# Attention in a hybrid decoder: another order of scores and turns, rotary angles on GpSimd, and x tiles between the first weights

## The chip, the cores and the metric

The kernel runs on one core of a Trainium2 chip. The metric is the device time of one execution in microseconds; the median of the runs is compared. A core has TensorE (PE in the profile), VectorE (DVE), ScalarE (ACT), GpSimd (POOL) and SyncE (SP). Each runs its own program in order, and semaphores make one wait for another. DMA transfers are issued from an engine's queue.

## The reference

Two layers over 512 positions of width 1024, all in float32. Layer 0 mixes by sliding-window attention, layer 1 by a gated delta rule; each is followed by a gated feed-forward part. The change lies in layer 0 alone:

```python
def swa_sink_attention(u, w_in, q_gain, k_gain, sinks, w_out, cos, sin):
    qkv = u @ w_in                                    # 16 query, 4 key, 4 value heads of 64
    q = partial_rope(rms_norm(q, q_gain), cos, sin)   # rotary on the first 16 of 64 dims
    k = partial_rope(rms_norm(k, k_gain), cos, sin)
    # blocks of 128 queries against their own and the previous block of keys, window 128
    scores = einsum("bnqhgd,bnkhd->bnhgqk", qb, kb) * (hd ** -0.5)
    probs = softmax(concatenate([masked scores, sink]))[..., :-1]
    return einsum("bnhgqk,bnkhd->bnqhgd", probs, vb) @ w_out
```

The angles of the rotary part are position times frequency, reduced to one period before the sine.

## The kernel before

**Matmuls.** A dense product in float32 is made of three matmuls (`mm3`, L148 to L150), with weights and activations each split in a rounded part and its remainder. `weight` loads a weight tile on SP's queue (L136), rounds it on ScalarE (L137, `whi`) and takes the remainder on VectorE (L138, `wlo`); there are three buffers of each. [...]

**Start.** `run` loads h in eight tiles of 128x512, h0 and h1 from ScalarE's queue and the others from SP's (L1131), and the first weight group W0 as four halves of 128x512, also from SP's. `norm_split` scales each tile by the gain on ScalarE (L192) and takes the remainder on VectorE (L193); squares for the normalisation follow on ScalarE (L180, L183). Some warm-up matmuls (L1128) stand ahead on TensorE.

**Attention.** `attn` runs six dense groups c = 0 to 5 over the weights win: c = 0 makes the keys, c = 3 the values, the others the queries of a key head each. Every group needs its own `weight` tiles. After the group its `post` normalises it and applies the rotary factors cc and sn (`qk_norm`), and turns it on TensorE (L427). The factors come from `attn_setup` and `rope`, called behind the dense loop of c = 0: 43 small instructions of 128x32 on VectorE between the cast of the positions and the sine, then three sine instructions on ScalarE (L332, L333) with a table load ahead.

**Lanes.** Two lanes, one behind the other, take two key heads each. For a block n of 128 queries and a key head, `attn_scores` makes the scores S of its four query heads on TensorE (L515), masks and maximises them on VectorE (L518), takes exponentials on ScalarE (L524), and scales them by the reciprocal sum, two heads on VectorE and two on GpSimd (L528). `attn_turn` turns these on TensorE (T, L537) and copies them to SBUF on ScalarE (L539). `attn_values` multiplies both heads' results with the values (V, L546). Block 0 has 128 keys, the others have 256. Lane 0 interleaves with the dense groups c = 2 to 5 and lane 1 with the output products of lane 0 (128x512).

**What sets the order.** The lanes are generators that the dense loops call by `pump`. A scheduler of the framework then gives each engine its final order by its own estimates, so that the program's order is not quite that of the code. DMAs from SP and ScalarE use eight semaphores in turn; the ninth waits until the first has landed.

Of the kernel before, what the change touches and what calls it, by code (L numbers as in the profile page):

```python
# [10 lines left out]
F32 = mybir.dt.float32  # L11
# [3 lines left out]
ALU = mybir.AluOpType  # L15
# [4 lines left out]
NB = 4  # L20
# [50 lines left out]
class Builder:  # L71
# [56 lines left out]
    def weight(self, src, cols=1024, parts=1):  # L128
# [134 lines left out]
    def rope(self):  # L263
        nc = self.nc
        n = NB * 8
        V = nc.vector
        new = lambda: self.ax.tile([P, n], F32, tag="ra", name="ra", bufs=10)
        pos = self.ax.tile([P, NB], I32, name="pos", bufs=1)
        nc.sync.dma_start(pos, self.ins["pos"])
        fr = self.ax.tile([P, 8], F32, name="fr", bufs=1)  # L270
        nc.sync.dma_start(fr, self.ins["freq"].partition_broadcast(P))
# [17 lines left out]
        def wrap(r, k):  # L289
            for cc in (c1, c2, c3):  # L290
                V.scalar_tensor_tensor(r, k, -cc, r, op0=ALU.mult, op1=ALU.add)

        def times(a, power):
            c = float(np.remainder(2.0 ** power, tp))
            if power == 22:
                c = 2.0 ** 22 - tp * np.floor(2.0 ** 22 / tp)
            hi = np.floor(c * 512) / 512
            mid = np.floor((c - hi) * 2 ** 21) / 2 ** 21
            k = nearest(a, c / tp)
            r = new()  # L300
            V.tensor_scalar(r, a, float(hi), None, op0=ALU.mult)
            V.scalar_tensor_tensor(r, k, -c1, r, op0=ALU.mult, op1=ALU.add)
            V.scalar_tensor_tensor(r, k, -c2, r, op0=ALU.mult, op1=ALU.add)
            V.scalar_tensor_tensor(r, a, float(mid), r, op0=ALU.mult, op1=ALU.add)
            V.scalar_tensor_tensor(r, k, -c3, r, op0=ALU.mult, op1=ALU.add)
            V.scalar_tensor_tensor(r, a, float(c - hi - mid), r, op0=ALU.mult, op1=ALU.add)
            return r
# [3 lines left out]
        V.scalar_tensor_tensor(B, A, -4096.0, ang, op0=ALU.mult, op1=ALU.add)  # L311
        a1 = nearest(A, 1.0 / 1024)
        a0 = new()
        V.scalar_tensor_tensor(a0, a1, -1024.0, A, op0=ALU.mult, op1=ALU.add)
# [81 lines left out]
    def attn(self, h, after):  # L396
# [38 lines left out]
        def lane(i):  # L435


            sc, pT = {}, {}
            for x in range(NB + 2):
                if x >= 2:  # L440
                    while "v" not in ready:
                        yield 0.5
                    n = x - 2
                    if n == 0:
                        ao[i] = [(self.a2(), self.a2()) for _ in range(4)]
                    po = self.psum()
                    both = [pT.pop((n, j)) for j in range(2)]
                    for b in range(len(both[0])):
                        for j in range(2):
                            self.attn_values(n, 2 * i + j, both[j], v, po, b)  # L450
                    for g in range(4):
                        s = slice(n * P, (n + 1) * P)
                        hi, lo = ao[i][g]
                        self.split(po[:, g * P:(g + 1) * P], hi[:, s], lo[:, s])
                    if n == NB - 1:
                        ready.add(("o", i))
                        return
                    yield 1
                for j in range(2):
                    kv = 2 * i + j  # L460
                    if x < NB:
                        while kv not in ready:
                            yield 0.5
                        sc[x, j] = self.attn_scores(x, kv, qT[kv], kT[kv])
                        yield 0.5
                    if 1 <= x < NB + 1:
                        pT[x - 1, j] = self.attn_turn(x - 1, sc.pop((x - 1, j)))
                        yield 0.5
# [4 lines left out]

        for c in range(6):
# [12 lines left out]
            if c == 0:  # L487
                self.attn_setup()
# [628 lines left out]
    def run(self, stages):  # L1117
# [12 lines left out]
        for m in range(KT):  # L1130
            (nc.scalar if self.first and m < 2 else nc.sync).dma_start(h[m], self.ins["xT"][m])  # L1131
            if self.first and m in (0, 1):
                self.W0 = (self.W0 if m else []) + [self.weight(self.ins["win"][0, m], 1024, 2)]
            if self.first:
                self.norm_split(h[m], m, gains[stages[0]])
            else:
                self.norm_tile(h[m], m, gains[stages[0]])
        nc.sync.dma_start(self.ident, self.ins["ident"])
# [39 lines left out]
```

## Time and profile before

| | us |
|---|---|
| median of three runs | 1492.2 (1490.68 to 1493.09) |
| profiled execution | 1490.9 |
| its span | 1489.0 |
| TensorE busy | 1468.6 |
| VectorE busy | 915.1 |
| ScalarE busy | 635.9 |
| GpSimd busy | 72.1 |

The span is the time from the first to the last record of the profile. TensorE is busy 99% of it, so the rows below look for the places where it is not.

### The profile page before, as it was taken

The numbers are of one execution on the slowest core, as the hardware profiler recorded it, in microseconds if no ns is written. First come the engines' busy times: TensorE is split into PE (matmuls) and PEld (weight loads), VectorE is DVE, ScalarE is ACT, GpSimd is POOL, SyncE is SP. The second block draws the span as 40 slices with busy tenths as digits, with TensorE's granted clock in tenths as the row PEclk, the third lists the DMA queues.
The fourth block names the chain that finished last, engine by engine and source line by source line (L and its number), as shares of the span: only waits on it lengthen the run. The fifth ranks groups of instructions, "written<-read, shape, count | busy, mean of one in ns | idle before, by whom it ended". The sixth has DMA issues, their size and how long they took to land.

```text
span 1489.0 us, 20841 instructions
## 1 busy us (share of the span) xinstructions
PE 1468.6 (99%) x7972; PEld 1217.8 (82%) x7972; DVE 915.1 (61%) x1772; ACT 635.9 (43%) x1206; POOL 72.1 (5%) x85
## 2 busy tenths in 40 slices
PE   8999999999999999999999999999999999999999
PEld 8976688888888888788877888888888888888887
DVE  8778766445535557764776676677685536544552
ACT  6666643223313343667534444454353313322331
POOL 0122100000000000000110111210000000000000
PEclk9999999999999999999999999999999999999999
DMA  5201222232322333356865555644232222233231
GB/s 187 72 20 60 84 97 98 97 99 99 100 98 87 99 125 123 124 179 228 280 223 174 148 152 170 162 140 139 71 99 99 99 93 93 97 99 99 97 106 66
DMA packets 84380, 178.14 MB, mean 120 GB/s; under 512 B 31544, under 2 KB 37688, under 8 KB 84024
## 3 DMA queue, kind: packets, MB, share of 16 engines
q1 hardware_dynamic: 76360, 160.54, 34.1%
q10 hardware_dynamic: 7920, 16.27, 2.9%
q8 instruction: 63, 1.03, 0.3%
q14 instruction: 37, 0.30, 0.1%
HBM read 150.46 MB, written 26.31 MB: 119 GB/s over the span
## 4 chain that ended last, share of the span: by engine, by line
PE 90%; DVE 4%; DMA 3%; ACT 2%; issue 1%; POOL 0%; SPq 0%; ACTq 0%; DVEq 0%
PE ps L148 27%; PE ps L150 26%; PE ps L149 26%; PE ps L574 1%; DMA z<-zd 1%; DVE wlo L138 1%; PE ps L515 1%; PE ps L546 1%; PE ps L1060 1%; PE ps L1073 1%; PE ps L1055 1%; PE ps L1051 1%; DMA vd<-t 1%; ACT sc L524 1%; PE ps L1066 1%
## 5 line engine op out<-in xcount | busy, mean ns | idle before, releaser
L148 PE MATMUL ps<-a,whi 128*128 128x512 f32 x1736 | 689.6, 397 | 3.9 <-ACT whi L137 3.5
L150 PE MATMUL ps<-a,wlo 128*128 128x512 f32 x1736 | 677.9, 391 | 0.5 <-DVE wlo L138 0.5
L149 PE MATMUL ps<-a,whi 128*128 128x512 f32 x1736 | 677.3, 390 | 0.0
L137 ACT CAST whi<-raw 128x1024 fp32r<-128x1024 f32 (+1 forms) x239 | 242.4, 1015 | 431.9 <-PE ps L149 386.6
L148 PEld LDWEIGHTS ps<-a,whi 128*128 128x128 f32 x1736 | 325.6, 188 | 73.6 <-ACT whi L137 3.9
L150 PEld LDWEIGHTS ps<-a,wlo 128*128 128x128 f32 x1736 | 325.5, 187 | 70.6 <-DVE wlo L138 1.0
L149 PEld LDWEIGHTS ps<-a,whi 128*128 128x128 f32 x1736 | 326.0, 188 | 64.3 <-DVE a L144 0.2
L138 DVE TENSOR_TENSOR wlo<-raw,whi 128x1024 fp32r<-128x1024 f32 (+1 forms) x239 | 281.5, 1179 | 81.0 <-ACT whi L137 79.1
L258 DVE TENSOR_TENSOR h<-h,ps 128x512 f32<-128x512 f32 x48 | 33.0, 688 | 148.5 <-PE ps L150 148.5
L243 DVE TENSOR_TENSOR t<-ps,rbc 128x512 f32<-128x512 f32 x48 | 33.2, 692 | 110.0 <-PE ps L150 103.9
L249 DVE TENSOR_TENSOR t<-ps,rbc 128x512 f32<-128x512 f32 x48 | 33.2, 692 | 86.4 <-PE ps L150 86.2
L247 ACT ACTIVATE t<-t 128x512 f32<-128x512 f32 x48 | 30.4, 632 | 97.8 <-DVE t L246 97.8
L148 PE MATMUL ps<-whi,a 128*128 128x256 f32 x192 | 57.3, 300 | 1.4 <-ACT a L192 1.2
L149 PE MATMUL ps<-wlo,a 128*128 128x256 f32 x192 | 54.3, 285 | 1.2 <-DVE wlo L138 1.2
L150 PE MATMUL ps<-whi,a 128*128 128x256 f32 x192 | 53.1, 283 | 0.0
L143 ACT CAST a<-t 128x512 fp32r<-128x512 f32 x48 | 29.9, 623 | 32.6 <-DVE t L250 32.6
L148 PEld LDWEIGHTS ps<-whi,a 128*128 128x128 f32 x192 | 36.9, 192 | 7.8 <-issue 4.9
L566 DVE SCALAR_TENSOR_TENSOR t<-ps,cols,t 128x511 f32<-128x511 f32 (+2 forms) x48 | 35.8, 745 | 6.2 <-ACT t L564 5.6
L244 ACT ACTIVATE t<-t,cols 128x512 f32<-128x512 f32 x48 | 38.9, 811 | 0.0
L149 PEld LDWEIGHTS ps<-wlo,a 128*128 128x128 f32 x192 | 36.9, 192 | 1.4 <-DVE wlo L138 1.4
L246 DVE SCALAR_TENSOR_TENSOR t<-t,cols,t 128x510 f32<-128x510 f32 x48 | 36.0, 750 | 1.7
L250 DVE TENSOR_TENSOR t<-t,t 128x512 f32<-128x512 f32 x48 | 33.2, 692 | 5.9 <-ACT t L247 0.8
(250 smaller groups left out, 1409.2 us busy)
## 6 DMA issues: line engine op xcount, KB each, us to landing
raw<-in_up SPq DMA_DIRECT2D x96, 512.0 KB, 3.3
raw<-in_down SPq DMA_DIRECT2D x48, 512.0 KB, 3.3
raw<-in_gin SPq DMA_DIRECT2D x48, 512.0 KB, 3.4
raw<-in_gout SPq DMA_DIRECT2D x16, 512.0 KB, 4.1
raw<-in_win SPq DMA_DIRECT2D x10, 512.0 KB, 3.3
raw<-in_wout SPq DMA_DIRECT2D x16, 256.0 KB, 2.7
zd<-t ACTq DMA_DIRECT2D x16, 256.0 KB, 2.6
Dd<-D ACTq DMA_DIRECT2D x8, 512.0 KB, 2.9
```

What stands on the lines that cost most here:

```text
L137: nc.scalar.copy(hi[:, s], raw[:, s])
L138: nc.vector.tensor_tensor(lo[:, s], raw[:, s], hi[:, s].bitcast(F32), op=ALU.subtract)
L148: mm(ps, w[0], x[0], start=first, stop=False)
L149: mm(ps, w[0], x[1], start=False, stop=False)
L150: mm(ps, w[1], x[0], start=False, stop=last)
L243: nc.vector.tensor_tensor(g, gu[0], self.bc, op=ALU.mult)
L244: nc.scalar.activation(y, g, AF.Identity, bias=self.col(C_FB + l * 24 + j), scale=self.col(cw + 2))
L246: nc.vector.scalar_tensor_tensor(y[:, 2:], g[:, :T - 2], self.col(cw), y[:, 2:], op0=ALU.mult, op1=ALU.add)
L249: nc.vector.tensor_tensor(t, gu[1], self.bc, op=ALU.mult)
L250: nc.vector.tensor_tensor(t, t, y, op=ALU.mult)
L258: nc.vector.tensor_tensor(h[m], h[m], ps, op=ALU.add)
L566: nc.vector.scalar_tensor_tensor(dst[:, i:], g[:, :T - i], self.col(cw + 3 - i), dst[:, i:], op0=ALU.mult, op1=ALU.add)
```

## The change

Three edits. **Lane order:** instead of a loop in which the score of block x and the turn of block x - 1 alternate for both heads, a list of steps: S(0,0), S(1,0), T(0,0), T(1,0), S(0,1), T(0,1), S(1,1), V(0), S(2,0), T(1,1) and so on, where the first index is the block and the second the head of the pair. **Rotary angles:** `rope` issues its two loads and all its arithmetic from GpSimd; each fused multiply-add becomes a product and a sum (`stt`). `attn_setup` is called before the dense loop of c = 0. **Start:** h0 to h3 are loaded from ScalarE's queue, and `norm_split` of the tiles stands between the weight halves.

```diff
+    def weight(self, src, cols=1024, parts=1, between=None):
             nc.vector.tensor_tensor(lo[:, s], raw[:, s], hi[:, s].bitcast(F32), op=ALU.subtract)
+            if between is not None:
+                between(i)
...
     def rope(self):
-        V = nc.vector
+        V = nc.gpsimd
+        def stt(o, x, c, y):
+            t = self.ax.tile([P, n], F32, tag="rb", name="rb", bufs=2)
+            V.tensor_scalar(t, x, c, None, op0=ALU.mult)
+            V.tensor_tensor(o, t, y, op=ALU.add)
+
-        nc.sync.dma_start(pos, self.ins["pos"])
+        nc.gpsimd.dma_start(pos, self.ins["pos"])
-        nc.sync.dma_start(fr, self.ins["freq"].partition_broadcast(P))
+        nc.gpsimd.dma_start(fr, self.ins["freq"].partition_broadcast(P))
...
         def wrap(r, k):
             for cc in (c1, c2, c3):
-                V.scalar_tensor_tensor(r, k, -cc, r, op0=ALU.mult, op1=ALU.add)
+                stt(r, k, -cc, r)
...
-            for x in range(NB + 2):
-                if x >= 2:
...
-                for j in range(2):
-                    kv = 2 * i + j
-                    if x < NB:
...
-                        sc[x, j] = self.attn_scores(x, kv, qT[kv], kT[kv])
-                        yield 0.5
-                    if 1 <= x < NB + 1:
-                        pT[x - 1, j] = self.attn_turn(x - 1, sc.pop((x - 1, j)))
-                        yield 0.5
+            S, T_, V_ = (lambda n, j: score(n, j)), (lambda n, j: turned(n, j)), values
+            for step in (S(0, 0), S(1, 0), T_(0, 0), T_(1, 0), S(0, 1), T_(0, 1), S(1, 1), V_(0), S(2, 0), T_(1, 1), S(2, 1),
+                         V_(1), T_(2, 0), S(3, 0), T_(2, 1), S(3, 1), V_(2), T_(3, 0), T_(3, 1), V_(3)):
+                yield from step
...
+        self.attn_setup()
         for c in range(6):
...
-            if c == 0:
-                self.attn_setup()
...
         for m in range(KT):
-            (nc.scalar if self.first and m < 2 else nc.sync).dma_start(h[m], self.ins["xT"][m])
-            if self.first and m in (0, 1):
-                self.W0 = (self.W0 if m else []) + [self.weight(self.ins["win"][0, m], 1024, 2)]
-            if self.first:
-                self.norm_split(h[m], m, gains[stages[0]])
+            (nc.scalar if self.first and m < 4 else nc.sync).dma_start(h[m], self.ins["xT"][m])
...
+            self.W0 = [self.weight(self.ins["win"][0, 0], 1024, 2, lambda i: i == 0 and self.norm_split(h[0], 0, G))]
+            for m in (1, 2):
+                self.norm_split(h[m], m, G)
+            self.W0.append(self.weight(self.ins["win"][0, 1], 1024, 2, lambda i: self.norm_split(h[3 + i], 3 + i, G)))
+            for m in (5, 6, 7):
+                self.norm_split(h[m], m, G)
```

What this does to the order of the engines is seen at three places. First SP's queue at the start of the program; `raw` is a half of the first weights, and h_85 to h_92 are the tiles h0 to h7. Before:

```order
L136 DMA raw<-in_win 128x512 x4
L1131 DMA h_87<-in_xT 128x512
L1131 DMA h_88<-in_xT 128x512 [waits DMAHW0_49]
L1131 DMA h_89<-in_xT 128x512 [waits DMAHW1_49]
L1131 DMA h_90<-in_xT 128x512 [waits DMAHW2_49]
```

and after:

```order
L1142 DMA h_89<-in_xT 128x512
L1142 DMA h_90<-in_xT 128x512
L1142 DMA h_91<-in_xT 128x512
L1142 DMA h_92<-in_xT 128x512
L136 DMA raw<-in_win 128x512 [waits DMAHW1_49]
L136 DMA raw<-in_win 128x512 [waits DMAHW2_49]
```

The four weight halves moved from the head of SP's queue behind h4 to h7, and each of them now waits for a DMA semaphore.

Second, ScalarE from the last squares of the start on; `cc` and `sn` are the rotary factors, a cast of 128x1024 is a weight tile of c = 1 or later, and L370 is a square of the keys behind c = 0. Before:

```order
L183 ACTIVATE t_182<-h_92 128x512 [waits DVE_49,PE_49]
L598 CAST identr<-ident 128x128 [waits DMAHW5_49]
L137 CAST whi<-raw 128x1024 [waits DMAHW7_49]
L370 ACTIVATE t_444<-ps 128x256 [waits PE_49] x2
L370 ACTIVATE t_448<-ps 128x256 [waits DVE_49,PE_49]
L137 CAST whi<-raw 128x1024 [waits DMAHW0_49]
```

and after:

```order
L185 ACTIVATE t_182<-h_92 128x512 [waits DVE_49,PE_49]
L340 ACT_TABLE_LOAD
L340 ACTIVATE cc<-ra 128x4x8 [waits Pool_49]
L340 ACTIVATE cc<-ra 128x4x8
L341 ACTIVATE sn<-ra 128x4x8
L137 CAST whi<-raw 128x1024 [waits DMAHW5_49]
L137 CAST whi<-raw 128x1024 [waits DMAHW6_49,DVE_49,PE_49]
```

The table load and the three sines moved from a place 8 rows further on, behind three such casts, to a place ahead of the first of them, with a wait for GpSimd.

Third, TensorE in lane 0, around the score of block 1 of the second head (keys a_189); L515 and L526 are scores, L537 and L548 turns, L557 value products. Before:

```order
L515 MATMUL ps<-a_189,a_911 128x256 x2
L515 MATMUL ps<-a_189,a_912 128x256 x2
L148 MATMUL ps<-whi,a_112 128x256
L149 MATMUL ps<-wlo,a_112 128x256
L150 MATMUL ps<-whi,a_113 128x256
L148 MATMUL ps<-whi,a_126 128x256
L149 MATMUL ps<-wlo,a_126 128x256
L150 MATMUL ps<-whi,a_127 128x256
L537 MATMUL ps<-ident,sc 128x128 x4
```

and after:

```order
L548 MATMUL ps<-ident,sc 128x128 x4
L526 MATMUL ps<-a_189,a_1002 128x256 x2
L526 MATMUL ps<-a_189,a_1003 128x256 x2
L557 MATMUL ps<-pT,v 64x512 x2
L526 MATMUL ps<-a_188,a_759 128x256 x2
L526 MATMUL ps<-a_188,a_760 128x256 x2
L152 MATMUL ps<-whi,a_157 128x256
L548 MATMUL ps<-ident,sc 128x128 x8
```

Before, the turn behind the score belongs to an earlier score of the same head (block 0). After, the eight turns at the end belong to the score at the head of the piece, with a value product, another score and one dense matmul in between.

## Rows read from the trace of the kernel before

**Rows 1.** The page, chain of waits: shares of the span by engine.

```profile
PE 90%; DVE 4%; DMA 3%; ACT 2%; issue 1%; POOL 0%; SPq 0%; ACTq 0%; DVEq 0%
```

**Rows 2.** Waits of TensorE, 0 to 220 us: in total, times, longest.

```profile
PE ps L537 <- DVE sc L528: 1.3, 1, 1.3
```

**Rows 3.** Windows: busy us and count of PE, PEld, DVE, ACT, POOL; clock, DMA share, GB/s.

```profile
20.00:30.00 10.00, 8.10 (x66) 7.69 (x66) 9.61 (x64) 3.65 (x8) 0.00 (x0) 1.00 0.44 133
140.00:160.00 20.00, 17.90 (x88) 10.06 (x88) 13.56 (x56) 15.45 (x53) 7.88 (x8) 0.94 0.15 41
```

**Rows 4.** Timeline of ScalarE at the start: start, length, what, idle before and releaser.

```profile
9.51 0.62 ACT L180 ACTIVATE t<-h 128x512 f32<-128x512 f32 x1
...
17.36 0.28 ACT L598 CAST identr<-ident 128x128 fp32r<-128x128 f32 x1
18.38 1.05 ACT L137 CAST whi<-raw 128x1024 fp32r<-128x1024 f32 x1 [0.73 <-DMA raw<-in_win]
...
33.01 0.35 ACT L332 ACTIVATE cc<-ra 128x32 f32<-128x32 f32 x2
```

**Rows 5.** Timeline of TensorE at the start.

```profile
6.27 0.58 PE L148 MATMUL ps<-whi,a 128*128 128x256 f32 x1
...
20.89 0.28 PE L148 MATMUL ps<-whi,a 128*128 128x256 f32 x1
22.37 0.38 PE L149 MATMUL ps<-wlo,a 128*128 128x256 f32 x1 [1.20 <-DVE wlo L138]
...
22.71 0.28 PE L148 MATMUL ps<-whi,a 128*128 128x256 f32 x1
22.83 0.28 PE L149 MATMUL ps<-wlo,a 128*128 128x256 f32 x1
```

**Rows 6.** Transfers, 0 to 25 us: GB/s in 40 slices; an issue, median us to landing.

```profile
GB/s 0 0 23 229 335 345 288 272 311 344 321 328 397 397 403 410 409 373 248 105 12 33 180 36 80 67 230 380 400 406 420 407 305 31 5 22 0 131 321 360
...
fr<-in_freq SPq DMA_DIRECT2D x1, 4.0 KB, 3.4
```

**Rows 7.** Groups of GpSimd by shape, whole span: busy us, mean ns, idle before.

```profile
L528 POOL TENSOR_SCALAR sc<-sc,sm 128x256 f32<-128x256 f32 x24 | 24.0, 1008 | 32.2 <-DVE es L521 7.3 <-ACT pT L539 6.5 <-DVE sm L526 6.3
...
L528 POOL TENSOR_SCALAR sc<-sc,sm 128x128 f32<-128x128 f32 x8 | 4.9, 625 | 96.6 <-DVE sm L526 59.4 <-DVE ss L169 18.0 <-DVE es L521 10.9
...
L898 POOL MEMSET X<- 128x64 f32 x1 | 0.2, 222 | 21.1 <-DVE X L896 21.1
```

**Rows 8.** Groups of VectorE by shape, 15 to 40 us: a step of the angles.

```profile
L291 DVE SCALAR_TENSOR_TENSOR ra<-ra 128x32 f32<-128x32 f32 x9 | 1.7, 194 | 0.0
```

**Rows 9.** Timeline of all engines at the end of lane 1.

```profile
148.93 1.14 PE L515 MATMUL ps<-a,a 64*128 64x256 f32 x8
...
150.21 0.48 DVE L518 CUSTOM_DVE_ANT_0 sc<-ps,band,rows 128x256 f32<-128x256 f32 x1 [0.48 <-PE ps L515]
...
153.37 0.51 ACT L524 ACTIVATE sc<-sc,nm 128x256 f32<-128x256 f32 x1 [0.65 <-DVE nm L520]
...
156.29 1.88 POOL L528 TENSOR_SCALAR sc<-sc,sm 128x256 f32<-128x256 f32 x2 [2.30 <-ACT pT L539]
...
157.33 0.75 PE L537 MATMUL ps<-ident,sc 128*128 128x128 f32 x3 [0.46 <-POOL sc L528]
...
159.27 2.83 PE L546 MATMUL ps<-pT,v 128*64 128x512 f32 x8
...
162.46 0.72 PE L148 MATMUL ps<-a,whi 128*128 128x512 f32 x2 [0.35 <-ACT a L143]
```

**Rows 10.** Timeline of TensorE in lane 0: scores, a value product, a turn.

```profile
50.63 0.72 PE L515 MATMUL ps<-a,a 64*128 64x128 f32 x8
...
65.40 1.13 PE L515 MATMUL ps<-a,a 64*128 64x256 f32 x8
...
79.90 1.04 PE L537 MATMUL ps<-ident,sc 128*128 128x128 f32 x8
...
81.58 1.98 PE L546 MATMUL ps<-pT,v 128*64 128x512 f32 x8
```

More of the change, by code (lines that the diff above doesn't have):

```diff
@@ L301, in times @@
             V.tensor_scalar(r, a, float(hi), None, op0=ALU.mult)
[L302 to L306, printed above, removed]
+            stt(r, k, -c1, r)
+            stt(r, k, -c2, r)
+            stt(r, a, float(mid), r)
+            stt(r, k, -c3, r)
+            stt(r, a, float(c - hi - mid), r)
             return r
@@ L310, in rope @@
         B = new()
[L311 removed]
+        stt(B, A, -4096.0, ang)
         a1 = nearest(A, 1.0 / 1024)
         a0 = new()
[L314 removed]
+        stt(a0, a1, -1024.0, A)
         kB = nearest(B, 1.0 / tp)
@@ L438, in lane @@
             sc, pT = {}, {}
-            for x in range(NB + 2):
-                if x >= 2:
-                    while "v" not in ready:
-                        yield 0.5
[L443 to L448, printed above, removed]
-                        for j in range(2):
[L450 to L457, printed above, removed]
-                    yield 1
-                for j in range(2):
-                    kv = 2 * i + j
-                    if x < NB:
-                        while kv not in ready:
-                            yield 0.5
-                        sc[x, j] = self.attn_scores(x, kv, qT[kv], kT[kv])
-                        yield 0.5
-                    if 1 <= x < NB + 1:
-                        pT[x - 1, j] = self.attn_turn(x - 1, sc.pop((x - 1, j)))
-                        yield 0.5
@@ new lines, in score, with turned, values @@
+            def score(n, j):
+                while 2 * i + j not in ready:
+                    yield 0.5
+                sc[n, j] = self.attn_scores(n, 2 * i + j, qT[2 * i + j], kT[2 * i + j])
+                yield 0.5
+            def turned(n, j):
+                pT[n, j] = self.attn_turn(n, sc.pop((n, j)))
+                yield 0.5
+            def values(n):
+                while "v" not in ready:
+                    yield 0.5
+                if n == 0:
+                    ao[i] = [(self.a2(), self.a2()) for _ in range(4)]
+                po = self.psum()
+                both = [pT.pop((n, j)) for j in range(2)]
+                for b in range(len(both[0])):
+                    for j in range(2):
+                        self.attn_values(n, 2 * i + j, both[j], v, po, b)
+                for g in range(4):
+                    s = slice(n * P, (n + 1) * P)
+                    hi, lo = ao[i][g]
+                    self.split(po[:, g * P:(g + 1) * P], hi[:, s], lo[:, s])
+                if n == NB - 1:
+                    ready.add(("o", i))
+                else:
+                    yield 1
@@ L1130, in run @@
         for m in range(KT):
-            (nc.scalar if self.first and m < 2 else nc.sync).dma_start(h[m], self.ins["xT"][m])
-            if self.first and m in (0, 1):
-                self.W0 = (self.W0 if m else []) + [self.weight(self.ins["win"][0, m], 1024, 2)]
-            if self.first:
-                self.norm_split(h[m], m, gains[stages[0]])
-            else:
-                self.norm_tile(h[m], m, gains[stages[0]])
+            (nc.scalar if self.first and m < 4 else nc.sync).dma_start(h[m], self.ins["xT"][m])
+            if not self.first:
+                self.norm_tile(h[m], m, gains[stages[0]])
+        if self.first:
+            G = gains[stages[0]]
+            self.W0 = [self.weight(self.ins["win"][0, 0], 1024, 2, lambda i: i == 0 and self.norm_split(h[0], 0, G))]
[4 more added lines that the diff above has]
+                self.norm_split(h[m], m, G)
         nc.sync.dma_start(self.ident, self.ins["ident"])
```

1 line of the change is left out of this document (removed).

## The prediction

> **What bounds the kernel now.** I read the page's chain of waits first: 90% of it is TensorE [rows 1]. So only idle time of TensorE, or time at its lower clock, can be gained or lost. Next come the waits of TensorE in the first 220 us; what this change touches there is 1.3 us in the last turn of lane 1 [rows 2] and 1.2 us on the low half of the second weight group [rows 5]. The windows show where such idling sits: 8.10 of 10 us busy at 20 to 30 us, 17.90 of 20 us at 140 to 160 us, there with a granted clock of 0.94 [rows 3]. After the attention the order of TensorE is unchanged, so whatever the change does is a shift of one instant: the first dense matmul behind the last value product of lane 1, which starts at 162.46 us [rows 9]. I look for what moves that instant, in two stages: the start (before the second weight group, c = 1) and the lanes.
>
> **The start: loads.** Before, the four halves of the first weights are first on SP's queue, and TensorE's first real matmul starts at 6.27 us [rows 5]. After, h4 to h7 stand ahead of these halves on SP's queue, and the first half waits for a slot that one of them frees; h0 to h3 load beside them. So nine tiles of 256 KB come before or with the first half. Adding up the slices of the transfer view (0.625 us each) reaches 9 x 262 KB = 2.36 MB at about 9.0 us [rows 6]. The first half lands at about 9.0 us (from 6 us, if SP's queue gets more than its share of the engines, to 9.7 us). From there ScalarE has 18 instructions before the table load: 4 casts, 7 scalings, 7 squares. Fourteen of this kind took from 9.51 to 17.36 us, 0.56 us each [rows 4], so 10.1 us: ScalarE ends them at 19 to 20 us where it ended at 17.36 us. TensorE starts c = 0 at about 9.8 us instead of 6.27 us and has 96 matmuls of 0.12 us (starts of 22.71 and 22.83 us, [rows 5]), 11.5 us if all of it ran without a wait, so c = 0 ends at 21.4 to 24 us, against about 20.9 us, where c = 1 begins [rows 5]. By itself this costs little: c = 1 waited until 22.37 us for its low half anyway [rows 5]. The cover is 1.5 us; the rest, 0 to 1.6 us, would show. That is the floor of this stage, +0.5 us.
>
> **The start: rotary angles.** This is where it turns. Before, the sine of the angles (33.01 us) stood on ScalarE behind the casts of c = 1, the first of which ran at 18.38 us [rows 4]. After, the three sine instructions stand AHEAD of the casts of c = 1, and wait for GpSimd. Queued behind that wait on ScalarE: both casts of c = 1, then VectorE's low halves, then all of c = 1 on TensorE. GpSimd's chain is: two loads issued at about 0.8 us, landed by about 4 us (3.4 us for the frequencies before [rows 6]), a cast, and 64 small operations of 128x32 one after the other (43 on VectorE before; 21 fused operations become two each). No row shows such an operation on GpSimd. Bounds: the same tile took VectorE 0.194 us [rows 8]; a fill of 128x64 took GpSimd 0.222 us; its scalings took 0.625 us for 128x128 and 1.008 us for 128x256 [rows 7]. A line through the last two gives 0.24 us + 0.003 us per column, 0.34 us at 32 columns; I take 0.335 us, since it is the same kind of instruction and lies between the fill and the scaling. That is 64 x 0.335 = 21.4 us, the chain ends at 25.4 us (16.5 us at 0.194, 44 us at 0.625). Then a sine row of 0.35 us for each of three, a cast of 1.05 us, and the low half of 1.2 us: c = 1 gets its low half at about 28.2 us instead of 22.37 us, +5.8 us; VectorE, relieved of 43 operations, gives some 0.7 us of the wait at the normalisation back. Step: **+5 us**, from +0.5 us (chain over by 20 us) to +16 us (0.5 us each).
>
> GpSimd stands idle for 59.4 us before its first tensor instruction [rows 7], so a cost of its first use, if there is one, could not be seen there; after, it would lie in the chain, because the order has one extra program instruction between the cast and the first product. [...]
>
> **The lanes.** What is computed stays; only TensorE's order changes. A turn needs its score's whole softmax. From the tail: a score that starts at 148.93 us ends at 150.07 us, its turn gets the last scaled part at 157.33 us, 7.3 us later [rows 9]. About 1.0 us of this is other heads' work on VectorE (first reduction 150.21 us, first exponential 153.37 us, where four reductions of 0.41 us and two small ones need 2 us), so 6.3 us is the least; narrow scores of block 0 are taken as 1.5 us shorter. Which turn waits is counted from the order: the TensorE work between a score and its own turn. Pieces, from start to next start and so a little under the busy times shown: dense 128x256 0.12 us [rows 5], 128x512 twice that, score 1.06 us, turn 0.8 us, value product 1.9 us [rows 10]. Before, 15 of the 16 turns have 5.3 us or more between; only the last has 3.5 us. After, in lane 0 the first head's block 1 has 4.7, the second head's block 1 only 2.1 (first value product, score of block 2, one matmul). In lane 1 the first head has 3.2 in block 0 and 1.8 in block 1, the second head 2.1 and 4.8, and the last turn 4.1. Walking the whole order with these pieces (stalls push later ones back) gives, at 6.3 us, stalls of 1.6, 4.2, 0.75 (last value product behind its copy) in lane 0 and 1.6, 2.9, 2.7, 1.5, 2.2, 0.75 in lane 1: 18 us after, against 3.8 us by the same walk before. At 7.3 us it is 25 against 6 us. Before really lost more: from 50.63 us [rows 10] to 162.1 us are 111.5 us, for 98.1 us of pieces; that is 13.4 us, since the idling of 154 to 158 us is followed by value products of 2.83 us where 1.9 us is normal [rows 9, 10], with a granted clock of 0.94 in that stretch [rows 3]. The tail of lane 1 is built alike in both, so I keep that extra in both. Step: **+14 us**; least +5 us (18 us against the 13.4 us measured), most +20 us. Early turns do not pay anything back: what they open (the value product) is behind the same copies.
>
> **Sum.** +5 and +14 are +19 us; the longer idling may hold the lower clock longer (20 us at 0.94 are 1.2 us [rows 3]), taken as 1 us. The profiled execution took 1490.9 us, so 1510.9 us; it lies 1.3 us under the median of 1492.2 us, so **1512 us** on the scale of the median.
>
> **Rivals.**
> (a) *GpSimd's chain is short*: operations at VectorE's 0.194 to 0.222 us, over by 18 us. Then the start costs +0.5 us, the lanes +5 to +14 us: 1498 to 1507 us. For it: the tiles are tiny. Against: 0.625 us at 128 columns.
> (b) *GpSimd's chain is long*: 0.43 to 0.5 us for each operation, or the same time lost at the head of the chain. It ends at 31 to 36 us, the start costs +11 to +16 us, the whole 1518 to 1523 us. For it: 0.625 us at 128 columns, and dependent operations that can't overlap. [...]
> (c) *The other side, faster*: the softmax latency falls with the new order, because VectorE and ScalarE are freer when TensorE runs ahead, and the early turns take the end of lane 1 (1.3 us of waits and the clock) away. With a latency of 4 us the walk's after-stalls fall to 6 us, under half of the 13.4 us measured before, and with the short chain of (a): 1492 - 7 + 0.5 = 1486 us. It decides from a latency under 4.5 us; four exponentials of 0.5 us and two scalings on GpSimd in 1.88 us [rows 9] leave hardly room, which is against it.
> (d) *The two shifts hide each other or vanish*: the c = 1 delay stays 0.5 us and lanes lose what they lost before: 1492 to 1495 us. For it: VectorE is 9.6 of 10 us busy at 20 to 30 us [rows 3] and gets relief. Against: TensorE waits in program order, and nothing behind makes up.
>
> **How the numbers follow.** My forecast (chain about 25 us, lanes +10 to +20 us) 0.42; (b) 0.23; (a) 0.18; (c) 0.08; (d) 0.09. A difference under 0.2% (3 us) is about what a measurement of this kernel cannot tell from none. The range leaves out (c), (d) up to 1496 us and beyond (b)'s 1523 us plus 5 us for the lanes' upper bound: 1497 to 1528 us. Faster by over 0.2%: (c), 0.08. Same: most of (d), 0.08. Slower: the rest, 0.84.
>
> **What would show it.** Right: TensorE idle from 6.1 to about 9.8 us, then a wait of 4 to 6 us for the first cast of c = 1, with ScalarE idle on GpSimd's chain until about 25 us; waits of turns (L548) on VectorE's and GpSimd's scalings of about 16 us in all, the longest 4 us, in lane 0 at the second head's block 1; the same TensorE record behind 162.46 us, moved by some 19 us. Wrong: GpSimd ending before 20 us (a), a gap before its first product (b), turns' waits under 8 us in sum (c, d), or differences behind the attention, which the order excludes.

## The result, and the profile after

The changed kernel takes 1537.6 us (1534.5 to 1543.1, four runs) against 1491.4 us; the ratio is 1.032, with a 95% interval of 1.029 to 1.035. The direction was forecast, the size was not: +46 us instead of +20 us, above the range of 1497 to 1528 us. The profiled execution has a span of 1534.1 us, 45.1 us more than before.

The page of the changed kernel, chain of waits by engine (answers to [rows 1]); TensorE lost three points and GpSimd, which had 0%, has two:

```profile
PE 87%; DVE 5%; POOL 2%; ACT 2%; DMA 2%; issue 1%; SPq 0%; ACTq 0%; POOLq 0%; DVEq 0%
```

The waits of TensorE up to 260 us (answers to [rows 2]; columns as there), and one of before that [rows 2] leaves out:

```profile
PE ps L150 <- ACT whi L137: 18.1, 2, 10.8
PE ps L548 <- DVE sc L539: 12.8, 7, 3.7
PE ps L548 <- POOL sc L539: 4.4, 11, 0.5
PE ps L548 <- DVE ss L171: 1.6, 1, 1.6
```

```profile
PE ps L537 <- POOL sc L528: 0.9, 2, 0.5
```

Where before turns waited once for VectorE's scaling (1.3 us) and twice for GpSimd's (0.9 us), they now wait seven times for VectorE's (12.8 us) and eleven times for GpSimd's (4.4 us), and there are 18.1 us in two waits for weight casts, of which before has none. The second of these casts stands behind the sines. ScalarE at the start (answers to [rows 4]) and TensorE (answers to [rows 5]):

```profile
11.99 0.62 ACT L137 CAST whi<-raw 128x512 fp32r<-128x512 f32 x1 [4.74 <-DMA raw<-in_win]
...
37.02 0.35 ACT L340 ACTIVATE cc<-ra 128x32 f32<-128x32 f32 x2 [13.12 <-POOL ra L336]
37.27 0.21 ACT L341 ACTIVATE sn<-ra 128x32 f32<-128x32 f32 x1
37.39 1.97 ACT L137 CAST whi<-raw 128x1024 fp32r<-128x1024 f32 x2
```

```profile
12.67 1.23 PE L150 MATMUL ps<-whi,a 128*128 128x256 f32 x4 [7.33 <-ACT whi L137]
...
38.47 0.58 PE L150 MATMUL ps<-whi,a 128*128 128x256 f32 x1 [10.78 <-ACT whi L137]
39.73 0.58 PE L151 MATMUL ps<-wlo,a 128*128 128x256 f32 x1 [0.68 <-DVE wlo L138]
```

ScalarE waits 13.12 us for GpSimd's last clamp, and c = 1 begins at 38.47 us instead of 20.89 us. The windows tell how much of the rest is waiting and how much a lower clock (answers to [rows 3]; columns as there):

```profile
10.00:20.00 10.00, 7.33 (x41) 7.33 (x42) 7.15 (x11) 7.64 (x14) 8.68 (x21) 0.60 0.78 276
...
30.00:40.00 10.00, 0.85 (x2) 0.56 (x3) 1.55 (x3) 2.98 (x8) 5.75 (x23) 0.59 0.00 0
...
100.00:110.00 10.00, 6.59 (x24) 4.19 (x26) 7.09 (x32) 6.19 (x23) 3.79 (x4) 0.67 0.00 0
```

Each of these stretches holds a wait of TensorE (7.33 us, 10.78 us, and 2.96 us ahead of a turn) and a granted clock of 0.59 to 0.67: it was 0.50 at 12 to 18 us, 34 to 45 us and 103.4 to 109.5 us, most of the stretch each time, and 1.00 at 46 to 60 us.

Three instants divide the 45.1 us. The first score of lane 0 is at 69.48 us, 50.63 us before [rows 10]: the start costs 18.9 us. From there to the first dense matmul behind the lanes, now at 206.72 us, are 137.2 us instead of 111.8 us [rows 9, 10]: the lanes cost 25.4 us. Behind it 0.8 us are left. The window from the first score to that matmul, TensorE alone (length, busy us and count, clock, DMA share, GB/s), first of before, then of after, last of a kernel below that has the new order almost without its waits (`no_scaling`):

```profile
50.63:162.46 111.83, 108.91 (x700) 0.98 0.15 43
```

```profile
69.48:206.72 137.24, 116.81 (x700) 0.94 0.11 35
```

```profile
50.77:163.03 112.26, 109.59 (x700) 1.00 0.13 41
```

Idle time went from 2.9 to 20.4 us (+17.5 us). Busy time, with the same 700 matmuls, went from 108.9 to 116.8 us (+7.9 us). Most of this is the clock: in the same order at a clock of 1.00 the work takes 109.6 us.

### The profile page after: what moved, and what is told of

It is laid out like the page before. It is cut to its first block, busy times and chain, and to the rows that moved or that the text cites. A ratio compares the mean times of both kernels' runs of the same rounds, so it can differ in the third digit from the quotient of the medians.

```text
span 1534.1 us, 20859 instructions
## 1 busy us (share of the span) xinstructions
PE 1482.8 (97%) x7972; PEld 1226.5 (80%) x7972; DVE 914.3 (60%) x1727; ACT 635.8 (41%) x1206; POOL 94.6 (6%) x153
## 4 chain that ended last, share of the span: by engine, by line
PE 87%; DVE 5%; POOL 2%; ACT 2%; DMA 2%; issue 1%; SPq 0%; ACTq 0%; POOLq 0%; DVEq 0%
PE ps L150 26%; PE ps L151 26%; PE ps L152 25%; PE ps L585 1%; ACT sc L535 1%; DVE wlo L138 1%; DVE sc L529 1%; POOL sc L539 1%; PE ps L1071 1%; PE ps L548 1%; PE ps L557 1%; PE ps L1084 1%; PE ps L1062 1%; PE ps L1066 1%; PE ps L526 1%
## 5 line engine op out<-in xcount | busy, mean ns | idle before, releaser
L150 PE MATMUL ps<-whi,a 128*128 128x256 f32 x192 | 58.7, 309 | 18.1 <-ACT whi L137 18.1
L150 PEld LDWEIGHTS ps<-whi,a 128*128 128x128 f32 x192 | 39.0, 205 | 23.0 <-ACT whi L137 18.7
L152 PE MATMUL ps<-whi,a 128*128 128x256 f32 x192 | 57.0, 297 | 0.0
L964 POOL MEMSET TT<- 128x1024 f32 x8 | 7.7, 960 | 569.5 <-DMA Xd<-kd 555.3
L548 PE MATMUL ps<-ident,sc 128*128 128x128 f32 x112 | 21.9, 309 | 20.1 <-DVE sc L539 12.8
L152 PEld LDWEIGHTS ps<-whi,a 128*128 128x128 f32 x192 | 39.3, 205 | 0.3 <-issue 0.3
```

The costliest lines, as they stand in the source:

```text
L150: mm(ps, w[0], x[0], start=first, stop=False)
L152: mm(ps, w[1], x[0], start=False, stop=last)
L548: nc.tensor.transpose(pt[:, g * P:(g + 1) * P], sc[:, g, b * P:(b + 1) * P], self.ident)
```

## The parts alone

The first four runs undo one part or do one part alone. The lane order taken back, in the changed kernel:

```diff
-            for step in (S(0, 0), S(1, 0), T_(0, 0), T_(1, 0), S(0, 1), T_(0, 1), S(1, 1), V_(0), S(2, 0), T_(1, 1), S(2, 1),
...
+            for x in range(NB + 2):
...
```

> The changed kernel with the old lane order (the loop in which score and turn alternate); rotary angles on GpSimd and the new start stay. Theory: the start and the lanes add up; the trace of after puts the start at +19.2 us (first score of lane 0 at 69.80 us, 50.63 us before) and the lanes at +25 us, so this kernel takes 1491 + 19 = about 1510 us and loses 25 to 28 us against after. Rival: the late start itself makes the lanes worse (clock, other engines out of step), then it lies nearer to before, 1500 us or less, or keeps part of the lanes' loss, over 1515 us.

Measured: 1510.9 us (1507.6 to 1513.3), ratio 1.013 (1.011 to 1.015). The first score is at 68.41 us, and the lanes take 112.2 us, nearly as before (111.8 us):

```profile
68.41:180.61 112.20, 109.07 (x699) 0.98 0.14 43
```

So the two stages add up, and the late start does not spoil the lanes.

The new lane order alone (the same diff the other way, in the kernel before):

> The kernel before with the new lane order alone. Theory (lanes and start add up): +25 us, about 1516 us. Rival (the walk of the prediction, +14 us, and the rest of the lanes' loss comes with the late start): about 1505 us. Rival (the new lane order is good where the start is not late): 1487 us or less.

Measured: 1522.1 us (1520.0 to 1527.9), ratio 1.021 (1.019 to 1.024), 5 us more than the larger theory. The same window (length, busy, clock, DMA share, GB/s):

```profile
50.78:194.91 144.13, 122.75 (x700) 0.88 0.12 34
```

The idle time is 21.4 us, nearly that of the changed kernel; the clock costs more here, 122.75 us of work against 108.9 us. The walk of the prediction, which had 18 to 25 us of stalls, was right about the idle time. The 14 us of slower work were not in it. They are those of the profiled execution, the slowest of the four (1527.9 us); the other three are 4 to 8 us faster, two of them with a mean granted clock of 0.989 over the whole execution instead of 0.984.

Rotary angles on GpSimd alone:

```diff
-        V = nc.vector
+        V = nc.gpsimd
...
-                V.scalar_tensor_tensor(r, k, -cc, r, op0=ALU.mult, op1=ALU.add)
+                stt(r, k, -cc, r)
```

> The kernel before with the rotary angles on GpSimd alone (loads from its queue, products and sums apart); the start's loads and the lane order are the old ones. Theory: the sine instructions stand ahead of the casts of c = 1 here too, and wait for GpSimd's chain, which ends at about 33 to 37 us; the second dense group starts 12 to 17 us late and the whole takes 1503 to 1509 us. Rival (the chain is long only since the new start delays or disturbs it): chain over by 26 us, +5 us, 1496 us.

Measured: 1510.1 us (1508.0 to 1512.4), ratio 1.013 (1.011 to 1.014). Here the wait ahead of c = 1 is one piece of 13.8 us:

```profile
36.13 0.58 PE L148 MATMUL ps<-whi,a 128*128 128x256 f32 x1 [13.80 <-ACT whi L137]
```

`attn_setup` is still called behind the dense loop of c = 0 in this kernel, and the sines stand ahead of the casts of c = 1 all the same. So the moved call is not what put them there.

The order of loads and casts alone:

```diff
-            (nc.scalar if self.first and m < 2 else nc.sync).dma_start(h[m], self.ins["xT"][m])
+            (nc.scalar if self.first and m < 4 else nc.sync).dma_start(h[m], self.ins["xT"][m])
...
+            self.W0 = [self.weight(self.ins["win"][0, 0], 1024, 2, lambda i: i == 0 and self.norm_split(h[0], 0, G))]
...
```

> The kernel before with the new order of loads and casts at the start alone. Theory: the first real matmul at about 12.7 us instead of 6.3 us, at the lower clock at first, c = 0 ends at 26 to 27 us instead of 20.9 us, of which the 1.5 us wait before c = 1 was cover: +4 to +6 us, 1496 us. Rival (the forecast's floor): +0.5 us, within 0.2%. Rival (the casts between the weights help): faster than before.

Measured: 1492.7 us (1491.3 to 1495.8), ratio 1.0009 (1.0000 to 1.0019), the forecast's floor of +0.5 us. I had revised it upward from the trace of after, wrongly: in that trace the cast of the first half was later still (first real matmul at 12.67 us, here at 10.07 us). In the profiled execution, the slowest of the ten, the first score is 2.5 us late (53.12 us); by the times, this part alone is worth nothing either way.

So the angles on GpSimd are worth +18 us, the lane order +25 to +30 us, and the start's order about nothing (0.6 us). The sum of the parts, 48 us, is near the whole, 46 us.

## Why the angles cost 18 us

The forecast had GpSimd's chain over at 25.4 us; in the changed kernel its last clamp begins at 36.77 us. Two pieces were wrong: it began at 9.96 us instead of 4 us, since the frequencies landed so late, and its 64 operations took 27 us instead of 21.4 us. GpSimd in the changed kernel (start, length, what):

```profile
9.96 0.23 POOL L283 TENSOR_TENSOR ra<-pf,fr 128x32 f32<-128x32 f32 x1 [4.00 <-DMA fr<-in_freq]
...
17.79 1.20 POOL L273 TENSOR_SCALAR rb<-ra 128x32 f32<-128x32 f32 x2
18.95 1.28 POOL L274 TENSOR_TENSOR ra<-rb,ra 128x32 f32<-128x32 f32 x2
...
31.49 0.66 POOL L273 TENSOR_SCALAR rb<-ra 128x32 f32<-128x32 f32 x2
32.11 0.58 POOL L274 TENSOR_TENSOR ra<-rb,ra 128x32 f32<-128x32 f32 x2
36.77 0.21 POOL L336 TENSOR_SCALAR ra<-ra 128x32 f32<-128x32 f32 x1
```

The same pairs take 1.2 us at 18 us and 0.6 us at 32 us. VectorE at 18 us is busy without a gap, with instructions of 128x512:

```profile
18.10 0.74 DVE L195 SCALAR_TENSOR_TENSOR a<-h,cols,a 128x512 fp32r<-128x512 f32 x1
18.76 0.69 DVE L186 TENSOR_TENSOR t<-t,t 128x512 f32<-128x512 f32 x1
```

At 32 us it has nothing to do. The next run leaves most of that work of VectorE out, in the kernel `lanes_old`: the remainders of the x tiles and the sums of the squares (`quiet` is set while these run).

```diff
-            nc.vector.tensor_tensor(self.acc, self.acc, sq, op=ALU.add)
+            if not getattr(self, "quiet", False):
+                nc.vector.tensor_tensor(self.acc, self.acc, sq, op=ALU.add)
...
-        nc.vector.scalar_tensor_tensor(lo, h, g, hi.bitcast(F32), op0=ALU.mult, op1=ALU.subtract)
+        if self.first and len(self.u) < KT and gain == C_MIX:
+            lo = hi
...
```

> The changed kernel with the old lane order, and with two kinds of VectorE operations at the start left out: the remainders of the x tiles (the rounded part stands in for it) and the sums of the squares; 15 operations of 0.7 us, only the four weight remainders stay. Theory: GpSimd's small operations take twice as long while VectorE works (starts 0.65 us apart instead of 0.33 us), so without that the chain of the angles ends at about 32 us instead of 37 us, and the time falls from 1511 us to 1504 to 1507 us. Rival: they were slow for another reason (the transfers, their own dependencies): the chain ends at 36 to 37 us, 1510 us.

Measured: 1505.1 us (1504.5 to 1506.4) against 1510.9 us. At 17 to 20 us the pairs now run at the fast rate, and the chain's last instruction, the negation behind the sines, is at 32.53 us. Last below is that instruction in `lanes_old`, at 37.38 us:

```profile
17.34 0.58 POOL L278 TENSOR_TENSOR ra<-rb,ra 128x32 f32<-128x32 f32 x2
18.00 0.66 POOL L277 TENSOR_SCALAR rb<-ra 128x32 f32<-128x32 f32 x2
...
32.53 0.29 POOL L346 TENSOR_SCALAR sn<-sn 128x32 f32<-128x32 f32 x1 [0.58 <-ACT sn L345]
```

```profile
37.38 0.29 POOL L342 TENSOR_SCALAR sn<-sn 128x32 f32<-128x32 f32 x1 [0.58 <-ACT sn L341]
```

The chain ends 4.85 us earlier, 0.1 us of which is an earlier start; the rest is GpSimd no longer slowed beside VectorE, and the time followed (5.8 us). In the changed kernel one of GpSimd's operations starts every 0.65 us while VectorE's, 0.69 to 0.74 us long, start 0.61 to 0.66 us apart, one for one. What of VectorE's work slows them, and how, is not shown. VectorE itself isn't slower, 0.74 us for a remainder of an x tile against 0.75 us before:

```profile
L193 DVE SCALAR_TENSOR_TENSOR a<-h,cols,a 128x512 fp32r<-128x512 f32 x8 | 6.0, 750 | 0.4 <-ACT a L192 0.4
```

The prediction had not looked at what VectorE does beside the chain.

Why the chain began late was asked by two runs. In the first, one tiny operation on GpSimd stands between the two loads, ahead of that of the frequencies:

```diff
+        nc.gpsimd.memset(pre, 0.0)
+        nc.gpsimd.tensor_scalar(pre[:, 1:2], pre[:, 0:1], 1.0, None, op0=ALU.mult)
```

> The kernel before with the rotary angles on GpSimd alone, and one tiny multiplication on GpSimd ahead of the second load of the angles, so that whatever the first tensor instruction on GpSimd costs is paid beside the loads. Theory (what GpSimd waits for until 8.4 us is the load of the frequencies): the first product still starts at 8 to 10 us, the time is 1510 us. [...]

Measured: 1507.7 us (two runs).

```profile
2.15 0.26 POOL L92 TENSOR_SCALAR pre<-pre 128x1 f32<-128x1 f32 x1
2.33 0.60 POOL L280 DMA_DIRECT2D fr<-in_freq  x1
5.86 0.18 POOL L282 CAST pf<-pos 128x4 f32<-128x4 int32 x1 [2.93 <-DMA pos<-in_pos]
8.75 0.24 POOL L284 TENSOR_TENSOR ra<-pf,fr 128x32 f32<-128x32 f32 x1 [2.71 <-DMA fr<-in_freq]
```

The first operation runs at 2.15 us for 0.26 us, and the first product still waits for the frequencies, until 8.75 us where it was 8.38 us. There is no first-use cost in that place. The time is 2.4 us lower although the chain starts no earlier; I have no cause for that from two runs. In the second, the loads go to the head of SP's queue:

```diff
+        nc.sync.dma_start(self.pos, self.ins["pos"])
+        nc.sync.dma_start(self.fr, self.ins["freq"].partition_broadcast(P))
         nc.scalar.dma_start(self.cols[:, :C_FCONV], self.ins["cols"][:, :C_FCONV])
```

> The kernel before with the rotary angles on GpSimd alone, but with the two loads of positions and frequencies at the head of SP's queue instead of on GpSimd's. Theory (the frequencies reach GpSimd at 8.4 to 10 us because their load goes through its own queue beside the start's 2.4 MB): the first product starts at 4 to 5 us, the chain ends 3 to 4 us earlier, about 31 us, and the time is 1505 to 1507 us instead of 1510 us. Rival (any load issued in the first microseconds is late beside the others): the first product at 7 us or later, 1509 us.

Measured: 1506.0 us (1504.7 to 1506.6), ratio 1.010 (1.008 to 1.011).

```profile
4.97 0.24 POOL L278 TENSOR_TENSOR ra<-pf,fr 128x32 f32<-128x32 f32 x1 [2.33 <-DMA fr<-in_freq]
```

The first product starts at 4.97 us, as the theory has it, and the load takes 3.6 us to land from its issue. In the changed kernel, from GpSimd's queue, it was issued at 2.01 us and took

```profile
fr<-in_freq POOLq DMA_DIRECT2D x1, 4.0 KB, 7.8
```

So the late start was that of this load. Whether GpSimd's queue made it slow or the 256 KB loads that were issued before it is not shown, since this run changed both. The chain ends only 2.3 us earlier (last clamp at 32.11 instead of 34.43 us), less than the 3 to 4 us expected, and the gain in time is of that size if each run is held against the kernel before measured beside it: 15.4 us slower than that here, 17.9 us with GpSimd's own queue.

The last question on this part is whether the place of the sines on ScalarE is the cost. They were tied to the third weight cast, that of the first weight of c = 2 (`W2`), so that they stand behind it. For this the edit also issues `W2` ahead of the loop of c = 1 and starts the keys' `post` there:

```diff
+            nc.scalar.activation(z, hi[:, 1023:1024].bitcast(F32), AF.Copy, scale=0.0)
+            for i in range(2):
+                nc.scalar.activation(self.cc[:, :, i], Cv, AF.Sin, bias=z)
...
+            if c == 1:
+                W2 = self.weight(self.ins["win"][2, 0])
+                self.sines(W2[0])
+                self.spawn(post(0, post0))
...
```

> The kernel before with the rotary angles on GpSimd alone, but with the sines tied to the third weight cast (a zero made from it is their bias), so that three casts stand ahead of them on ScalarE instead of behind. Theory: what costs 18 us is the place of the sines on ScalarE, not the work on GpSimd: c = 1 starts at 21 to 22 us as before, what then waits for the sines at 35 us is the normalisation of the keys and the fourth cast, and 1492 to 1498 us are left. Rival: c = 1 or the keys' turn waits for GpSimd's chain in any case: 1503 us or more.

Measured: 1504.2 us (1503.1 to 1505.4), ratio 1.009 (1.008 to 1.011). My theory falls halfway: no cast of c = 1 waits for the sines any more, but 6 of 18 us are all that this saves. The two waits that took the place of the old one are behind the sines, which run at 38.06 us here, too:

```profile
42.38 0.58 PE L148 MATMUL ps<-whi,a 128*128 128x256 f32 x1 [4.32 <-ACT whi L137]
47.56 0.58 PE L149 MATMUL ps<-wlo,a 128*128 128x256 f32 x1 [4.60 <-DVE wlo L138]
```

The first is the fourth cast behind the sines on ScalarE. The second is a weight remainder behind the keys' rotary steps on VectorE, which wait for the sines. With the loads first as well:

> As the run before, with the sines tied to the third weight cast as in the run that tied them there (1504 us, whose chain ended at 38 us and whose later casts and normalisations still waited). Theory: what is left of the start's loss is the length of the chain against the 33 us at which the sines ran before; with the chain over by about 31 to 33 us it is 1492 to 1496 us. [...]

Measured: 1501.3 us (1500.5 to 1502.3), ratio 1.007 (1.006 to 1.008). It is 5 us above the range of my theory: the angles cost with the sines behind the casts, too. The sines run at 35.11 us here, since the chain takes 30.0 us instead of 27.1 us with the loads first alone: two pairs of GpSimd's operations take 1.44 and 1.50 us from 24.27 us, there 0.66 and 0.58 us. In the last kernel below, the same with other lanes, they take 1.60 and 1.50 us from 24.61 us, and VectorE is busy for 4.72 us of the 5 us from 25 us. Before, the sines ran at 33.01 us [rows 4]. The first score is at 58.77 us, 8.1 us late. The waits of TensorE for remainders and casts:

```profile
PE ps L149 <- DVE wlo L138: 4.0, 2, 3.3
PE ps L148 <- ACT whi L137: 2.7, 2, 1.7
```

Of the two waits behind the sines, 3.3 us for the remainder and 1.0 us for the fourth cast are left, if the longer wait for a cast, 1.7 us, is at the start. I put it there since the three kernels with the loads at the head of SP's queue, ahead of the weight halves, have two waits for a cast each, one of them of 1.6 to 2.3 us, and the other three with the angles on GpSimd and the old order of the start and the lanes have one. The first squares of the keys behind c = 0 start at 21.35 us instead of 19.34 us, and the second cast of c = 1 at 23.24 us instead of 21.02 us. So some 2 of the 8.1 us are lost before the sines matter, and some 6 us behind them.

## Why the lanes cost 25 to 30 us

The theory is that a turn waits whenever the order puts less TensorE work between a score and its turn than the softmax takes, and that TensorE's clock falls behind such waits. First the latency: the scaling left out, in the new order and in the old.

```diff
-        for g in range(4):
-            (nc.gpsimd if g % 2 else nc.vector).tensor_scalar(sc[:, g, :W], sc[:, g, :W], sm[:, g:g + 1], None, op0=ALU.mult)
```

> The kernel with the new lane order alone, with the scaling of the exponentials by the reciprocal sum left out (two operations on VectorE and two on GpSimd for each score), so that a turn follows the last exponential; nothing else is left out. Theory: the waits are the latency of the softmax against the work that the order puts between a score and its turn, and this cuts about 2 us from each of some nine waits, and most of the lower clock with them: the waits of turns fall from 20 to 8 to 11 us, the time from 1522 us to 1502 to 1507 us. Rival: the turns wait for something else (banks, copies, ScalarE's queue): 1515 us or more.

> The kernel before with the scaling of the exponentials left out, the same edit as in the run with the new lane order, as its base. Theory: before, turns wait for 2.2 us in all, so this gains at most those and the lower clock behind them: 1487 to 1491 us, and without the scaling the two lane orders are within 3 us of each other. Rival (leaving the scaling out frees engines and gains in any order): 1480 us or less.

Measured: 1491.4 us in the new order (1489.3 to 1493.8) instead of 1522.1 us, and 1487.9 us in the old (1486.1 to 1490.7). So the two orders differ by 3.4 us without the scaling, by 30 us with it. I had expected 8 to 11 us of waits to remain; 2.1 us remain:

```profile
PE ps L539 <- ACT sc L528: 2.1, 5, 1.5
```

So the turns waited for their own score's softmax, up to its last step, and not for banks or copies. My 2 us for the scaling's share of it were too few: without it a turn no longer waits for the sum, its reciprocal, and their places in the queues of VectorE and GpSimd either. In the changed kernel the latency is nearly as before, 7.0 us against 7.3 us: the score that starts at 96.47 us ends at 97.6 us, and GpSimd ends its last scaled part at 104.6 us, with TensorE idle for 2.96 us ahead of the turn.

Then the clock. Idle matmuls ahead of the turns that waited longest fill the waits:

```diff
...
+            for _ in range(0 if b else warm):
+                nc.tensor.matmul(pt[:, :2 * P], self.ident, self.band, start=True, stop=True)
             for g in range(4):
                 nc.tensor.transpose(pt[:, g * P:(g + 1) * P], sc[:, g, b * P:(b + 1) * P], self.ident)
```

> The kernel with the new lane order alone, plus idle work: ahead of the seven turns that waited longest stand 3 to 10 extra matmuls of 128x256 (47 in all and some more, about 14 us at the full clock) into the bank that the turn overwrites. They compute nothing that is used. Theory: of the 32 us that the lanes cost there, 18 us are TensorE idling for the softmax and 14 us the lower clock that follows the idling; the extra matmuls lie inside the waits and hold the clock, so the time falls from 1522 us to 1508 to 1512 us though work was added. Rival: the lower clock doesn't come from the idling, or the extra work lies on the path: 1522 us or more, up to 1536 us.

Measured: 1523.7 us (1520.5 to 1526.9), so by the time this run decides nothing: the extra matmuls took 25.8 us of busy time instead of 14 us, more than the waits that they filled (idle time fell from 21.4 to 8.1 us), and pushed turns that were ready. With fewer:

> The kernel with the new lane order alone with fewer idle matmuls ahead of the turns that wait: 28 of 128x256, each 0.46 us by the last trace (the estimate of 0.27 us for the last such kernel was too low, its 53 took 24 us and were longer than the waits), 13 us in all. Theory: they lie inside 21 us of waits, hold the clock, and the lanes lose the waits alone: 1522 us falls to 1508 to 1513 us. Rival: the lower clock costs nothing by itself, and the time stays at 1520 us or more.

Measured: 1516.1 us (1515.2 to 1519.4), 6 us under the order without them, though 28 matmuls were added. The window of the lanes (columns as above) and the group of the extra matmuls in it (two records for each):

```profile
53.39:187.77 134.38, 124.52 (x756) 0.99 0.12 36
```

```profile
L541 PE MATMUL ps<-band,ident 128*128 128x256 f32 x56 | 13.3, 381 | 0.0
```

Without the extra ones the work takes 124.5 - 13.3 = 111.2 us instead of 122.75 us, at a clock of 0.99 instead of 0.88. The lanes are 9.7 us shorter than without the extra matmuls; the profiled run's first score was 2.6 us later at the start, where TensorE waited 3.1 instead of 1.6 us for the first x tiles, and the time fell by 6 us instead of the 9 to 14 us expected. So the lower clock follows the waits, and about 11 us of the 32 us that the lanes cost in the profile without the extra matmuls are its part. It does not follow every wait: in the changed kernel it fell behind three of them (2.96, 3.71 and 1.74 us ahead of the turns at 103, 153 and 200 us), to a granted clock of 0.50 at 103.4 to 109.5, 153 to 158 and 203 to 205 us, not behind one of 1.84 us at 172 us (1.00 from 165 to 180 us); with the new lane order alone it fell at five places, one of them behind a wait of 1.82 us at 156 us (0.79 from 160 to 170 us, with dense matmuls of 128x512 that start 0.43 us apart at 163 us and 0.23 us apart at 166 us).

Last, an order by the theory's rule: both heads two blocks ahead, so that every turn has enough work behind its score.

```diff
+            for step in (S(0, 0), S(0, 1), S(1, 0), S(1, 1), T_(0, 0), S(2, 0), T_(0, 1), S(2, 1), V_(0), T_(1, 0), S(3, 0), T_(1, 1), S(3, 1), V_(1), T_(2, 0), T_(2, 1), V_(2), T_(3, 0), T_(3, 1), V_(3)):
...
```

> The kernel before with another list of lane steps: both heads of a pair run two blocks ahead of their turns (S(0,0), S(0,1), S(1,0), S(1,1), T(0,0), S(2,0), T(0,1), S(2,1), V(0), T(1,0), S(3,0), T(1,1), S(3,1), V(1), T(2,0), T(2,1), V(2), T(3,0), T(3,1), V(3)). Theory (a turn waits where the work between its score and itself is less than the softmax latency): here the walk of the prediction gives 1.6 us of stalls at a latency of 6.3 to 7.3 us, against 3.8 to 5.9 us before and 18 to 25 us in the changed kernel, so the time is 2 to 4 us under before, 1487 to 1490 us. Rival (running ahead itself is harmful: it crowds banks, buffers and the softmax of two heads into each other): slower than before.

Measured: 1490.3 us (1488.7 to 1493.3), ratio 0.9988 (0.9979 to 0.9997), 2 us under the kernel before. It is the only complete kernel here that is under both, by a margin that these runs (eleven against twenty-one) can just tell from none. No turn waits for a scaling in it, and the lanes take 110.2 us instead of 111.8 us at a clock of 1.00:

```profile
50.82:161.06 110.24, 108.08 (x700) 1.00 0.15 44
```

With the angles on GpSimd, loads first and sines behind:

> As the run before, with both heads of a pair two blocks ahead in the lanes (1490.3 us alone, 2 us under before). Theory: the gains and losses add up, 1490 to 1494 us; it beats both kernels only if the angles on GpSimd cost nothing any more. Rival: the lanes' order turns bad with VectorE's and GpSimd's other timing, 1500 us or more.

Measured: 1498.0 us (1496.7 to 1499.3), ratio 1.005 (1.004 to 1.006). It is 3 us under the same kernel with the old lanes, so the lanes' gain adds here too, but the angles on GpSimd and the loads that they need early keep costing.

## The prediction, point by point

- *The start: loads.* Its mechanism and floor held: alone, 1492.7 us. Its first half was cast at 9.40 us there, as forecast; in the changed kernel at 11.99 us, but GpSimd's chain hid that.
- *The start: rotary angles.* The mechanism held: the sines stand ahead of the casts, and ScalarE waits 13.12 us for GpSimd. The step that failed is the length of GpSimd's chain: over at 25.4 us in the sum, at 37.0 us in the trace. So the term was mis-sized, +5 us for +18.9 us, the largest error in the sum. Half of it is the load of the frequencies (landed at 9.9 us, not 4 us: I took a landing of SP's queue for one of GpSimd's), half the operations, 0.42 us each on average: my 0.335 us was right while VectorE is idle, 0.65 us holds beside VectorE. One slip cancels: I wrote 0.35 us for each of three sines, where [rows 4] has that for two together; the 28.2 us that follows goes by the row. Rival (b) had the place and named neither cause.
- *The lanes.* The walk's stalls, 18 to 25 us, held: 20.4 us of idle time (21.4 us alone), though the longest is 3.7 us in lane 1 and the place that the prediction named has 2.96 us. But for the least of the range the sum lost it again: from 98.1 us of pieces I made a loss of 13.4 us before. The pieces were too short; the same work at a clock of 1.00 is 107.8 us busy (the kernel with only the start's order, below), so the kernel before lost some 4 us, and the least of +5 us was no bound.

```profile
53.12:164.01 110.89, 107.78 (x699) 1.00 0.14 44
```

- *The clock* is the second step that failed, and by its ratio the worst: +1 us in the sum, +7.9 us of busy time in the lanes. Behind the late start there is more of it: from 40.1 to 45.2 us, at a granted clock of 0.50 up to 45 us, the matmuls of c = 1 start 0.21 us apart instead of 0.12 us, and from the first matmul of c = 1 to the first score are 31.0 us instead of 29.7 us. I had a row for the clock behind 2.1 us of idling, 1.2 us lost [rows 3], and did not scale it to the 14 us of the forecast, which would have been 8 us.
- *Rivals.* (a), (c) and (d) are out: no chain was over before 31 us, the latency is 7.0 us in the one place where it was read, and neither shift vanished. The view that showed it best was the one named at the end: TensorE idle to c = 1 with ScalarE on GpSimd, and turns waiting at L548.

By the terms: start 18.9, idle lanes 17.5, slower work in the lanes 7.9, rest 0.8, in sum 45.1 us; forecast 5, 14, 1 and 0. Of the 25 us that the forecast was short, the start is 13.9 us and the clock 6.9 us.

## What to carry over

Count the work between a producer and its consumer on the engine that bounds the kernel, for every pair in the order, before and after: where it falls under the latency of the path outside, the difference was idle time here, and in the changed kernel the lower clock added nearly half as much again (7.9 us to 17.5 us). A chain that is moved to an idle engine is not free (+18 us here): ask in which queue its consumer stands and what is queued behind it, when its data lands, and what VectorE does meanwhile. Taking one operation out of the latency (the scaling) is a quick test of whether an order is latency-bound.

## What the runs showed of the hardware

- In the changed kernel GpSimd's operations of 128x32 start 0.33 us apart from 26.2 to 36.8 us, where VectorE is idle, and 0.65 us apart from 15.9 to 24.3 us, beside VectorE instructions of 128x512 (0.69 to 0.74 us) without a gap. With most of these left out, pairs at 17 to 19 us take 0.58 to 0.66 us instead of 1.20 to 1.28 us. VectorE isn't slowed (0.74 us against 0.75 us before).
- A 4 KB load from GpSimd's queue at the start of the changed kernel, issued at 2.01 us behind other loads, took 7.8 us to land; the same load at the head of SP's queue took 3.6 us.
- The lower clock that followed waits cost up to two thirds of the waits again: in the slowest execution with the new lane order alone, 21.4 us of idle time came with 122.75 us of work where the kernel before has 108.9 us, 13.8 us more; in the changed kernel 20.4 us came with 7.9 us more.
